# Batched x·yᵀ in fp32: two of twelve loads issued among the stores, and the first four result tiles placed after loads 6 to 9

## The chip, the core and the metric

The kernel runs on one core of a Trainium2 chip. The metric is the device time of one execution in microseconds; the time before is 301.36 us, the median of 3 runs (301.17 to 301.5). The engines of the core that matter here are PE (matmul), ACT (ScalarE), DVE (VectorE), POOL (GpSimd) and SP (SyncE, which only issues transfers here); 16 DMA engines move data between the device's memory and the core's own.

## The reference

```python
def setup_inputs():
    batch, n_heads, seq_t, seq_s, channels = 8, 12, 512, 512, 64
    return {
        "x": np.random.randn(batch, n_heads, seq_t, channels).astype(np.float32),
        "y": np.random.randn(batch, n_heads, seq_s, channels).astype(np.float32),
    }

def reference(x, y):
    return np.einsum('bhtc,bhsc->bhts', x, y).astype(np.float32)
```

For each of the 96 pairs of batch and head (called heads below) it is the product of a 512 x 64 matrix with the transpose of another, 512 x 512 out. The inputs are 12.6 MB each, the output is 100.7 MB.

## The kernel before

**Tiling.** The 96 heads are cut into six groups of 16 (`NG`, `G`). x of one group is 2 MB, and so is y of one group; each is one load of 128 partitions x 4096 fp32. There are twelve loads, numbered n = 0 to 11: even n is x of group n // 2, odd n is y of that group, so loads 10 and 11 are x and y of the sixth group. A group is worked in two halves of 8 heads (i = 0 to 11, `NH`), a half in four result tiles of 2 heads (o = 0 to 47, `V` = 4 tiles in a half). A result tile is again 128 x 4096 fp32, 2 MB, and is stored with one transfer.

**Slots.** All 60 transfers, loads and stores alike, go through five buffers of 2 MB, `slot0` to `slot4`. `slot()` (line 131) hands them out in turn, in the order in which the program asks, so whoever asks takes the buffer that was handed out five requests before, and has to wait until that one's use is over: a load waits for the conversions of the load before it or for the store before it, an eviction likewise.

**From a load to a tile.** `compress(n)` (line 144) converts a load to bf16 and frees its slot. For x it is one ACT instruction over the whole slot (line 121). For y it is four quarters in the order of `in_front` (line 116): DVE, POOL, DVE, ACT. `mix(i, name, part)` (line 168) spreads x of half i over the block layout `xbs`, four parts, and `transposes(i)` (line 183) turns `xbs` and the y copy on DVE into `xT` and `yT`, which PE multiplies. There are two of each of `xbs`, `xT` and `yT`, one for even halves and one for odd.

**Results.** `result(o, s)` (line 242) makes tile o in slot s: PE fills two PSUM buffers, `pms[0]` and `pms[1]`, with four matmuls each, and ACT evicts each of them into one half of the slot (line 249). Then the tile is stored: by SP at once, or, where `by_act(o)` (line 229) holds (every third tile and the last four), by ACT. A store by ACT is put aside in `later` and is issued between the two evictions of the next tile (lines 256 to 258), so that ACT's queue does not stand still for it.

**Order.** Every engine runs its instructions in the order in which the program emits them; `emit` (line 92) works out the semaphore waits from what is read and written. `all_products` gives PE the same order of tiles in a loop, so PE is held only by ACT's evictions and DVE's transposes. The order of the front is the loop of line 285 over n, one round per load: `compress(n)`, one part of a `mix` on POOL, a further load in the rounds 0 to 4, and so on. Loads 0 to 4 are issued ahead of it. The slots of the front come out so:

| what asks | slot | freed by |
|---|---|---|
| loads 5 to 9 | 0 to 4 | conversion of loads 0 to 4 |
| tile 0 (asks in round 5, made in round 8) | 0 | conversion of load 5 |
| load 10 (round 6) | 1 | conversion of load 6 |
| tile 1 (asks in round 7, made in round 9) | 2 | conversion of load 7 |
| load 11 (round 8) | 3 | conversion of load 8 |
| tile 2 (asks in round 9, made in round 10) | 4 | conversion of load 9 |
| tile 3 (round 11, ahead of the conversion of load 11) | 0 | store of tile 0 |

After the front comes the loop of line 303 over tiles 4 to 47, which calls `prepare(i)` (line 264) behind the last tile of each half: the transposes for the half after next, and on DVE the four parts of `mix` for the one after that.

Of the kernel before, what the change touches and what calls it, by code (L numbers as in the profile page):

```python
# [9 lines left out]
def kernel(  # L10
# [31 lines left out]
    V = G // 4  # L42
# [3 lines left out]
    SLOTS = 5  # L46
# [45 lines left out]
    def emit(name, make, reads=(), writes=(), dma=None, lane=None, known_by=None):  # L92

        points = [writer[r] for r in (*reads, *writes) if r in writer]
        points += [v for w in writes for v in readers.get(w, ())]
        if name == "pool" and name in ticks:
            points.append((name, ticks[name]))
        need(name, points, known_by)
        p, step = (lane or name, 1) if dma is None else (f"dma{dma}", 16)
        if p not in sems:  # L100
            sems[p] = tc.alloc_semaphore(p)
        if make is not None:
            make().then_inc(sems[p], step)
        at = (p, ticks.get(p, 0) + step)
        ticks[p] = at[1]
        snaps[at] = {**known[name], p: at[1]}
        if dma is None:
            for q in lanes.get(name, (name,)):
                snaps[at][q] = ticks.get(q, 0)
        for r in reads:  # L110
            readers.setdefault(r, []).append(at)
        for w in writes:
            writer[w], readers[w] = at, []
# [4 lines left out]
    def copy(name, dst, src, reads, writes):  # L118
        emit(
            name,  # L120
            lambda: nc.scalar.activation(dst, src, COPY)  # L121
            if name == "act"
            else engines[name].tensor_copy(dst, src),  # L123
            reads,
            writes,
        )

    def both(i):
        return [("slot", i, 0), ("slot", i, 1)]

    def slot():
        made_slots.append(len(made_slots) % SLOTS)
        return made_slots[-1]

    def load(n):
        i = loaded[n] = slot()
        emit(
            "sp",
            lambda: nc.sync.dma_start(slots[i], (yv if n % 2 else xv)[n // 2]),  # L139
            writes=both(i),  # L140
            dma=i,
        )

    def compress(n):

        i = loaded.pop(n)
        g = n // 2
        if n % 2 == 0:
            xk = g % (NG - 1)
            dst = xks[xk].rearrange("p r c -> p (r c)")  # L150
            copy("act", dst, slots[i], both(i), [("xk", xk)])
            return
        ys = slots[i].rearrange("p (r c) -> p r c", c=C)
        for half in range(2):
            b = g % (NG - 1 + half)
            yv2 = ybs[half][b].bitcast(bf16).rearrange("p (j c w) -> p j w c", j=R // 2, w=2)
            for ch in range(2):
                copy(
                    in_front[2 * half + ch],
                    yv2[ch * 64:(ch + 1) * 64],  # L160
                    ys[half * 64:(half + 1) * 64, :, ch * D:(ch + 1) * D].rearrange(
                        "p (j w) c -> p j w c", w=2
                    ),
                    both(i),
                    [("yb", half, b, ch)],
                )

    def mix(i, name, part):

        g, half = divmod(i, 2)  # L170
        ch, u = divmod(part, 2)
        lo = half * 64 + u * D
        xk = g % (NG - 1)
        xv2 = xbs[half].bitcast(bf16).rearrange("p (k e c u) -> p k e c u", k=K, e=E, u=2)
        copy(
            name,
            xv2[part * D:(part + 1) * D, :, :, :, u],
            xks[xk][lo:lo + D, :, ch * D:(ch + 1) * D].rearrange("p (e k) c -> p k e c", k=K),
            [("xk", xk)],
            [("xb", half, part)],  # L180
        )

    def transposes(i):
        g, half = divmod(i, 2)
        b = g % (NG - 1 + half)
        emit(
            "dve",
            lambda: nc.vector.transpose(  # L188
                xTs[half].rearrange("p (k r e) -> p k e r", k=K, e=E),
                xbs[half].rearrange("p (k e c) -> p k e c", k=K, e=E),  # L190
            ),
            [("xb", half, part) for part in range(4)],
            [("xT", half)],
        )
        emit(
            "dve",
            lambda: nc.vector.transpose(  # L197
                yTs[half].rearrange("p (r j) -> p j r", r=D),
                ybs[half][b].rearrange("p (j c) -> p j c", c=D),
            ),  # L200
            [("yb", half, b, ch) for ch in range(2)],
            [("yT", half)],
            lane="tr",
        )

    def products(o, k):
        evicted = 2 * o + k // 4 + 1
        emit("pe", None, [("xT", o // V % 2), ("yT", o // V % 2)], [("pm", k // 4)],
             known_by=[("ev", evicted), ("tr", o // V + 1)])
# [19 lines left out]
    def by_act(o):  # L229
        return o % 3 == 2 or o >= V * NH - V  # L230

    def store(o, s):
        i, h = divmod(o, V)
        name = "act" if by_act(o) else "sp"
        emit(
            name,
            lambda: engines[name].dma_start(ov[i, h], slots[s]),
            reads=both(s),
            dma=s,
        )  # L240

    def result(o, s):

        for k in range(0, K, 4):
            pm = k // 4
            products(o, k)
            emit(
                "act",
                lambda: nc.scalar.activation(  # L249
                    slots[s][:, k * S:(k + 4) * S], pms[pm].rearrange("p j s -> p (j s)"), COPY  # L250
                ),
                [("pm", pm)],
                [("slot", s, pm)],
                lane="ev",
            )
            if k == 0:
                while later:
                    store(*later.pop())
        if by_act(o):
            later.append((o, s))  # L260
        else:
            store(o, s)

    def prepare(i):

        if i < NH:
            transposes(i)
        if i + 1 < NH:
            for part in range(4):
                mix(i + 1, "dve", part)  # L270

    with tc.tile_critical():  # L272
        sems["ev"] = tc.alloc_semaphore("ev")
        ticks["ev"] = 2
        nc.scalar.sem_inc(sems["ev"], 2)
        for g in range(SLOTS):
            load(g)
        for half, name in enumerate(("dve", "pool")):
            emit(
                name,  # L280
                lambda: engines[name].memset(xbs[half], 0.0),  # L281
                writes=[("xb", half, part) for part in range(4)],
            )
        front = []
        for n in range(2 * NG):
            if n == 11:
                result(3, slot())
            compress(n)
            mix(n // 4, "pool", n % 4)
            if n == 4:  # L290
                transposes(0)
            if n < 5:
                load(n + SLOTS)
            elif n in (6, 8):
                load(n // 2 + 7)
            elif n < 10:
                front.append(slot())
            if n > 7 and n < 11:
                result(n - 8, front[n - 8])
            if n == 9:  # L300
                transposes(1)
        prepare(2)
        for o in range(V, V * NH):
            result(o, slot())
            if o % V == V - 1:
                prepare(o // V + 2)
        store(*later.pop())
        all_products()
        for i, name in enumerate(("dve", "pool", "dve", "pool", "act")):
            need(name, [(f"dma{i}", ticks[f"dma{i}"])])  # L310
# [30 lines left out]
```

## Time and profile before

| | us |
|---|---|
| median of 3 runs | 301.36 |
| the profiled execution | 301.07 |
| its span, first to last instruction | 299.2 |
| ACT busy (109 instructions) | 210.8 |
| DVE busy (73) | 151.8 |
| PE busy (384 matmuls) | 127.0 |
| POOL busy (23) | 56.1 |
| ACT, one eviction of half a tile (x96) | 1.884 |
| ACT, conversion of x (x6) | 3.617 |
| ACT, a quarter of y (x6) | 2.462 |
| DVE, a quarter of y (x12) | 3.018 |
| POOL, a quarter of y (x6) | 2.973 |

125.85 MB are moved, at 421 GB/s over the span. The transfers on SP's queue take 69.3% and those on ACT's queue 29.6% of the time of all 16 DMA engines. The median time from the issue of a transfer to its landing is 16.6 us for a store by SP, 14.7 us for a store by ACT, 17.5 us for a load of x and 20.8 us for a load of y, where one of these transfers alone is a few microseconds of the engines' time: most of it is waiting behind others. A row of a timeline gives the start, the busy time, the engine, the line, the operation with what it writes and reads, and in brackets the idle time before it and what ended that. Neighbouring instructions of one kind are merged in a row ("x2"), with their busy time added up.

### The profile page before, as it was taken

What the parts mean: (1) busy time and instruction counts of PE and PEld (TensorE: products, weight loads), DVE (VectorE), ACT (ScalarE), POOL (GpSimd) and SP (SyncE); (2) the same over time, 40 slices, a digit from 0 to 9 for tenths busy, and PEclk for the clock granted to TensorE, in tenths of its full rate; (3) what the DMA queues carried; (4) which work ended last, traced back from release to release, by engine and by line L of the source; (5) the groups of instructions that cost most, each with busy time, mean ns of one, the idle gap of its engine ahead of it and who ended that gap; (6) DMA issues with size and microseconds to landing.
All of it is one profiled execution on the core that took longest, in us unless ns stands there. A gap on an engine that the chain in (4) does not pass through costs nothing.

```text
span 299.2 us, 1282 instructions
## 1 busy us (share of the span) xinstructions
PE 127.0 (42%) x384; PEld 34.5 (12%) x384; DVE 151.8 (51%) x73; ACT 210.8 (70%) x109; POOL 56.1 (19%) x23
## 2 busy tenths in 40 slices
PE   0000040546666554565554556454646454736000
PEld 0000010111111111111111111111111111111000
DVE  2257897999839592920946729229276340000000
ACT  1665576999999886767686868585959595959400
POOL 2399999991000000000000000000000000000000
PEclk9999999958799979695979595979595979596855
DMA  7999999999999999999999999999999999999995
GB/s 274 427 431 429 434 423 429 431 429 431 429 434 429 429 431 435 425 431 436 429 431 428 434 429 429 434 425 434 434 423 427 425 434 427 425 423 429 431 429 223
DMA packets 8642, 125.85 MB, mean 421 GB/s; under 512 B 960, under 2 KB 960, under 8 KB 960
## 3 DMA queue, kind: packets, MB, share of 16 engines
q1 hardware_dynamic: 6048, 88.08, 69.3%
q10 hardware_dynamic: 2592, 37.75, 29.6%
q14 instruction: 2, 0.02, 0.0%
HBM read 25.17 MB, written 100.66 MB: 420 GB/s over the span
## 4 chain that ended last, share of the span: by engine, by line
DMA 57%; ACT 23%; PE 6%; issue 6%; DVE 2%; SPq 0%; ACTq 0%
DMA out_dram<-slot 44%; ACT slot L249 20%; DMA slot<-in_y_dram 7%; DMA slot<-in_x_dram 6%; PE pm L223 6%; DVE yb L123 2%; ACT xk L121 1%; ACT yb L121 1%; SPq L139 0%; ACTq L85 0%; SPq L336 0%; SPq L272 0%
## 5 line engine op out<-in xcount | busy, mean ns | idle before, releaser
L249 ACT ACTIVATE slot<-pm 128x2048 f32<-128x2048 f32 x96 | 173.2, 1884 | 46.9 <-DMA out_dram<-slot 43.9
L223 PE MATMUL pm<-yT,xT 128*128 128x512 bf16 x384 | 127.0, 470 | 150.5 <-ACT slot L249 113.4
L188 DVE STREAM_TRANSPOSE xT<-xb 128x2048 uint32<-128x2048 uint32 x12 | 46.7, 3890 | 71.5 <-PE pm L223 69.1
L223 PEld LDWEIGHTS pm<-yT,xT 128*128 128x128 bf16 x384 | 34.5, 111 | 242.5 <-ACT slot L249 170.9
L123 DVE COPY xb<-xk 32x2048 bf16<-32x2048 bf16 x36 | 46.9, 1303 | 1.0
L123 DVE CAST yb<-slot 64x2048 bf16<-64x2048 f32 x12 | 36.2, 3018 | 16.7 <-DMA slot<-in_y_dram 16.5
L123 POOL COPY xb<-xk 32x2048 bf16<-32x2048 bf16 x12 | 36.2, 3019 | 10.3 <-ACT xk L121 9.5
L121 ACT ACTIVATE xk<-slot 128x4096 bf16<-128x4096 f32 x6 | 21.7, 3617 | 16.1 <-DMA slot<-in_x_dram 16.1
L197 DVE STREAM_TRANSPOSE yT<-yb 128x1024 uint32<-128x1024 uint32 x12 | 23.1, 1925 | 0.0
L121 ACT ACTIVATE yb<-slot 64x2048 bf16<-64x2048 f32 x6 | 14.8, 2462 | 5.1 <-DMA slot<-in_y_dram 5.1
L123 POOL CAST yb<-slot 64x2048 bf16<-64x2048 f32 x6 | 17.8, 2973 | 1.3 <-DMA slot<-in_y_dram 0.8
L281 DVE MEMSET xb<- 128x2048 uint32 x1 | 1.8, 1765 | 1.4 <-SPq L272 1.4
L121 ACT ACT_TABLE_LOAD x1 | 1.3, 1283 | 1.0 <-SPq L272 1.0
L281 POOL MEMSET xb<- 128x2048 uint32 x1 | 1.8, 1806 | 0.5 <-SPq L272 0.5
L325 POOL MEMSET const-float32-0.0<- 128x1 f32 x1 | 0.1, 98 | 0.2 <-issue 0.2
L325 POOL MEMSET const-float32-1.0<- 128x1 f32 x1 | 0.1, 98 | 0.0
L325 POOL MEMSET const-bfloat16-1.0<- 128x1 bf16 x1 | 0.1, 98 | 0.0
L325 POOL MEMSET const-uint8-127<- 128x1 uint8 x1 | 0.1, 98 | 0.0
## 6 DMA issues: line engine op xcount, KB each, us to landing
out_dram<-slot SPq DMA_DIRECT2D x30, 2048.0 KB, 16.6
out_dram<-slot ACTq DMA_DIRECT2D x18, 2048.0 KB, 14.7
slot<-in_x_dram SPq DMA_DIRECT2D x6, 2048.0 KB, 17.5
slot<-in_y_dram SPq DMA_DIRECT2D x6, 2048.0 KB, 20.8
```

What stands on the lines that cost most here:

```text
L121: lambda: nc.scalar.activation(dst, src, COPY)
L123: else engines[name].tensor_copy(dst, src),
L188: lambda: nc.vector.transpose(xTs[half].rearrange("p (k r e) -> p k e r", k=K, e=E), xbs[half].rearrange("p (k e c) -> p k e c", k=K, e=E),),
L197: lambda: nc.vector.transpose(yTs[half].rearrange("p (r j) -> p j r", r=D), ybs[half][b].rearrange("p (j c) -> p j c", c=D),),
L223: last = nc.tensor.matmul(pms[pm][:, b, :], xT[:, 4 * pm + b, h, :], yT[:, h * S:(h + 1) * S], start=True, stop=True,)
L249: lambda: nc.scalar.activation(slots[s][:, k * S:(k + 4) * S], pms[pm].rearrange("p j s -> p (j s)"), COPY),
L281: lambda: engines[name].memset(xbs[half], 0.0),
L325: nc = _bacc.Bacc("TRN2", target_bir_lowering=False, num_devices=1)
```

## The change

Loads 10 and 11 leave the front. Rounds 6 to 9 of the front each make one of tiles 0 to 3, right behind the conversion of that round's load, in slots 0 to 3. Rounds 10 and 11 keep only their part of `mix` on POOL. In the loop over the tiles, load 10 is issued ahead of tile 16 and converted ahead of tile 20, and load 11 is issued ahead of tile 26 and converted ahead of tile 30; each takes a turn among the slots. Tile 20 is made in the slot of load 10, and tile 30 in the slot of load 11.

```diff
-        front = []
         for n in range(2 * NG):
-            if n == 11:
-                result(3, slot())
-            compress(n)
+            if n < 10:
+                compress(n)
             mix(n // 4, "pool", n % 4)
             if n == 4:
                 transposes(0)
             if n < 5:
                 load(n + SLOTS)
-            elif n in (6, 8):
-                load(n // 2 + 7)
-            elif n < 10:
-                front.append(slot())
-            if n > 7 and n < 11:
-                result(n - 8, front[n - 8])
+            if n > 5 and n < 10:
+                result(n - 6, slot())
             if n == 9:
                 transposes(1)
         prepare(2)
         for o in range(V, V * NH):
+            for n, at in ((10, 4 * V), (11, 6 * V + 2)):
+                if o == at:
+                    load(n)
+                if o == at + SLOTS - 1:
+                    compress(n)
             result(o, slot())
```

## The prediction, made before the changed kernel had run

> **What bounds the kernel now.** I read the slices first, then the engine rows at the place that the diff touches. In the slices, DMA is the busy share of the 16 transfer engines and GB/s what they moved, in 40 slices of 7.48 us.
>
> ```profile
> DMA  7999999999999999999999999999999999999995
> GB/s 274 427 431 429 434 423 429 431 429 431 429 434 429 429 431 435 425 431 436 429 431 428 434 429 429 434 425 434 434 423 427 425 434 427 425 423 429 431 429 223
> HBM read 25.17 MB, written 100.66 MB: 420 GB/s over the span
> L249 ACT ACTIVATE slot<-pm 128x2048 f32<-128x2048 f32 x96 | 173.2, 1884 | 46.9 <-DMA out_dram<-slot 43.9
> ```
>
> The reader is to see that no slice between the first and the last is below nine tenths, at about 429 GB/s, whether it holds loads (the first eight) or stores (the rest). A transfer of 2 MB (2.097 MB) at 429 GB/s is 4.89 us, and 60 of them are 293.4 us of the 299.2 us span; the remaining 5.8 us lie before the first packet and after the last. Transfers are the bound from end to end, and ACT, the busiest engine, waits 43.9 us for stores to free slots. The byte count does not change, so the question is only whether the engines ever run dry in the new order. There is nothing to gain inside the stream, as it has no hole.
>
> Next the rows of the front: ACT's, then DVE's from two windows (the two casts of load 7 together, which follow the last cast of load 5 on that engine; then the second of them alone, and the first of load 9), and SP's first two issues.
>
> ```profile
> 33.00 2.48 ACT L121 ACTIVATE yb<-slot 64x2048 bf16<-64x2048 f32 x1 [1.27 <-DMA slot<-in_y_dram]
> 37.90 3.62 ACT L121 ACTIVATE xk<-slot 128x4096 bf16<-128x4096 f32 x1 [2.41 <-DMA slot<-in_x_dram]
> 42.79 2.45 ACT L121 ACTIVATE yb<-slot 64x2048 bf16<-64x2048 f32 x1 [1.28 <-DMA slot<-in_y_dram]
> 47.69 3.62 ACT L121 ACTIVATE xk<-slot 128x4096 bf16<-128x4096 f32 x1 [2.44 <-DMA slot<-in_x_dram]
> 51.21 3.63 ACT L249 ACTIVATE slot<-pm 128x2048 f32<-128x2048 f32 x2
> 54.86 2.46 ACT L121 ACTIVATE yb<-slot 64x2048 bf16<-64x2048 f32 x1
> 57.35 3.65 ACT L249 ACTIVATE slot<-pm 128x2048 f32<-128x2048 f32 x2
> 61.02 3.62 ACT L121 ACTIVATE xk<-slot 128x4096 bf16<-128x4096 f32 x1
> 64.54 3.63 ACT L249 ACTIVATE slot<-pm 128x2048 f32<-128x2048 f32 x2
> 68.38 1.88 ACT L249 ACTIVATE slot<-pm 128x2048 f32<-128x2048 f32 x1 [0.21 <-PE pm L223]
> 68.39 0.66 ACTq L237 DMA_DIRECT2D out_dram<-slot  x1
> ```
>
> ```profile
> 43.36 6.88 DVE L123 CAST yb<-slot 64x2048 bf16<-64x2048 f32 x2
> ...
> 46.79 3.45 DVE L123 CAST yb<-slot 64x2048 bf16<-64x2048 f32 x1
> 52.59 1.33 DVE L123 CAST yb<-slot 64x2048 bf16<-64x2048 f32 x1 [2.34 <-DMA slot<-in_y_dram]
> ```
>
> ```profile
> 0.96 0.39 SPq L139 DMA_DIRECT2D slot<-in_x_dram  x1
> 1.41 0.42 SPq L139 DMA_DIRECT2D slot<-in_y_dram  x1
> ```
>
> The ACT rows that waited for a load started when it landed: load 6 at 37.90, load 7 at 42.79, load 8 at 47.69, 4.89 us apart. The store of tile 2 (by_act, line 230) goes out on ACT's queue, and line 256 puts it behind the first eviction of tile 3: it was issued at 68.39, 0.01 us after that eviction began at 68.38. This is the step on which the case turns.
>
> **The change part by part.** (1) Loads 10 and 11 leave the front. By the slices the first eight hold 3278 GB/s x 7.48 us = 24.52 MB at 59.84 us. Twelve transfers are 25.17 MB; the missing 0.65 MB take 1.5 us, so the twelfth ends at 61.35 us. Before, that twelfth transfer is load 11 and the store of tile 0 follows it without a hole. After, the first twelve are ten loads and the stores of tiles 0 and 1, and the store of tile 2 has to be in the queue by 61.35. The tenth ends 9.78 us earlier, at 51.6, the eleventh at 56.5.
>
> (2) The first tiles move ahead, each behind one conversion on ACT. I follow ACT with the durations above. Tile 0 goes into slot 0, which DVE's second cast of load 5 frees; it ends as the first cast of load 7 begins, at 43.36 (ACT is free from load 6 at 41.52). Then: tile 0 43.4 to 47.0 (3.63); ACT's quarter of load 7, 2.45, to 49.5; tile 1, 3.65, to 53.1; load 8, 3.62, to 56.75; tile 2, 3.63, to 60.4; ACT's quarter of load 9, 2.46, to 62.9; first eviction of tile 3 at 62.9. Slot 1 was freed by ACT itself, slot 2 by DVE's last cast of load 7 at 46.79 + 3.45 = 50.2, slot 3 by ACT: no wait there. PE refills a buffer in at most 1.9 us after its eviction, and between two evictions of one buffer lie 3.6 us and more: no wait there either. So tile 0's store is issued at 47.0, tile 1's at 53.1, tile 2's not at 60.4, when it is complete, but at 62.9.
>
> (3) How long an issue needs to become traffic in an empty queue is shown once, at the start. SP's first issue begins at 0.96; in quarter-microsecond windows the first packets lie in 1.75 to 2.00, so 1.05 us. The windows 2 to 4 moved 262 GB/s and not 429, which is another 0.78 us lost: 1.82 us until the effective full rate. Store 0 (47.0 against 51.6) and store 1 (53.1 against 56.5) are in time by either. Store 2 becomes traffic at 62.9 + 1.05 = 63.95 or, with the ramp, at 64.75. **The hole is 63.95 - 61.35 = 2.6 us to 64.75 - 61.35 = 3.4 us.** I take 3.0, the middle, as a store's ramp is not shown and ACT's issue instruction is longer than SP's (0.66 against 0.39).
>
> Beside the row stands a rule: the Trainium skill, DMA: Bandwidth & Descriptors, Specifications, gives about 0.6 us from issue to first byte for transfers issued by SP and ACT. By it the hole would be 62.9 + 0.6 - 61.35 = 2.15 us; the one start that this trace shows took 1.05 us, and I keep that.
>
> (4) After the hole. Tile 3's second eviction ends at 66.65 and its store (SP) is issued then, with first packets at 67.7; store 2 runs to at least 68.8. Tile 4 needs DVE's transposes of the second half, which in the trace end at 61.16 + 1.97 = 63.1 and depend on nothing that moves; PE refills after tile 3's first eviction (64.8 + 1.9), ACT evicts 66.9 to 70.5, and its store's packets can begin at 71.6, against 73.7. From there ACT makes a tile in 3.65 us and the engines take 4.89 for one, so the queue deepens by 1.2 us per tile and the wait is back on the transfers. The margin is thinnest at store 3, 1.1 us.
>
> (5) POOL loses its cast of load 11 (2.46) in the front, DVE its two casts there (6.62 us), ACT 3.62 and 2.50 us. They come back in the loop. All of it is beside the transfers, before and after, and saves nothing.
>
> (6) Load 10 in the loop, ahead of tile 16. It takes a slot as soon as that slot's store has landed, 0.33 us of SP's time, in SP's queue ahead of store 16, whose slot comes free only later; nothing on SP is held up. ACT converts it (3.62) ahead of tile 20, so what is queued behind that wait on ACT is tile 20's eviction and store, and all after. Four stores (16 to 19) stand behind the load when it lands. Count three of them to be safe: 14.7 us, less 1.5 us as a landing comes after its packets (load 0's packets end, with the ramp, near 2.8 + 4.9 = 7.7 and ACT starts on it at 8.57; 1.5 is on the safe side), 13.2 us of cover. The conversion and tile 20's two evictions take 7.3, and packets follow at 8.3 or 9.1. It costs nothing, with 4 us to spare.
>
> (7) Load 11 ahead of tile 26: DVE casts two quarters, POOL one, ACT one, ahead of tile 30. On DVE the casts stand behind the transposes and four copies for the next halves (3.9 + 1.9 + 4 x 1.3 = 11.1 us), which start when PE is through tile 27, some 10 us before the load lands: up to 2 us late. A cast is 1.33 us with POOL quiet and 3.45 beside it, so 2.7 to 6.9 us; I take 4.8, as load 9's two together were. Slot free after at most 2 + 6.9, store 30 issued 3.65 later at 12.6, against 13.2 by three stores and 18 by four. The cost is nothing at the value taken (10.5), and at the far end 12.6 + 1.8 - 13.2 = 1.2 us.
>
> (8) The tail has the same 60 uses of the five slots, the last four stores on ACT's queue, and ACT idle after 280 us: nothing moves but the whole.
>
> Sum: +3.0 us against the profiled execution's 301.07 us (span 299.2): 304.1. The median of the runs shown, 301.36, lies 0.29 above that execution, so I predict **304.3**.
>
> **The rivals.** *No hole, time as before.* This needs store 2 in the queue by 60.3, when it becomes traffic at 61.35; ACT would have to be 2.6 us earlier at tile 3. The one wait in the chain is tile 0's for slot 0, 1.84 us from 41.52 to 43.36; were that cast quicker by all of it (load 9's first took 1.33), 0.75 us of hole remain by the lower bound, 302.1. To vanish, the issue on ACT's queue would also have to pass the conversion of load 9 ahead of it, as it needs only the evictions; at 60.4 it would be traffic at 61.45 and the time 301.4. Against it: at 68.39 the issue came with the eviction that follows, not at 68.17 where tile 2's evictions ended. Chance 0.09.
>
> *A second hole in the loop* at load 10 or 11, from the point where the wait for a converted slot outlasts the stores behind it. For it: both conversions stand ahead of an eviction in ACT's order. Against: 4 us of spare in (6), 0 to 7 in (7), and ACT's 43.9 us of waiting. Price 1.2 us by (7), and 4.9 if a store more is missing: 305.5 to 309.2. Chance 0.12.
>
> *Faster, through loads that run beside stores.* Before, all loads come first; if a read and a write together moved more, two loads of some 20 us each in the queue would gain. For it: nothing. Against: the slices of loads (423 to 434) and of stores (423 to 436) are alike, and the slice where they meet, the ninth, is 429. At the best slice's 436 the gain is 40 us x 7/429 = 0.65 us, which leaves 303.6; to end below 301.36 the pair would need 8% more, 463 GB/s. Chance of ending faster 0.03.
>
> **How the numbers follow.** One hole, 2.0 to 4.0 us (the bounds 2.6 and 3.4, with the rounding of the drain and of ACT's chain, 0.6, on both sides): 303.4 to 305.4, chance 0.76. A measurement of this kernel tells 0.2%, 0.6 us, from no change. The 0.09 without a full hole split into same 0.07 and slower 0.02; so faster 0.03, same 0.07, slower 0.76 + 0.12 + 0.02 = 0.90. The range reaches down to the quick-cast case at 302.1, rounded up to 302.4, and up to 306.2, over the 1.2 us of (7): about 0.17 lie outside it.
>
> **What would show it.** In the changed profile: tile 0's eviction at 43.4; two evictions and one conversion in turn on ACT; the first issue on ACT's queue at 62.9, not 68.39; the 2 us windows between 61.4 and 64.4 nearly empty where before they move 418 to 434 GB/s; all slices after that at 429; the ACT rows after 280 us of before about 3 us later; no empty window where loads 10 and 11 are converted. I am wrong if the windows from 61 to 65 are full, or if the hole is there and the end does not move, or if a window in the loop is empty.

## The result, and the profile after

The changed kernel takes 303.80 us (median of 4 runs, 303.62 to 303.91) against 301.33 for the kernel before in the same series: a ratio of 1.0082, 95% interval 1.0069 to 1.0094. It is 2.47 us slower. The profiled execution has a span of 301.8 us against 299.2.

From the page of the changed kernel, the slices (7.545 us each now) and ACT's evictions:

```profile
DMA  7999999989999999999999999999999999999995
GB/s 278 421 441 423 426 443 413 428 341 449 419 417 436 432 416 417 447 352 415 421 441 423 436 432 422 441 423 439 426 432 434 423 439 423 434 434 421 443 423 252
HBM read 25.17 MB, written 100.66 MB: 417 GB/s over the span
L249 ACT ACTIVATE slot<-pm 128x2048 f32<-128x2048 f32 x96 | 173.0, 1892 | 46.2 <-DMA out_dram<-slot 39.5
```

The bytes are the same, and ACT still waits for stores. Two slices are low, not one: the ninth (60.4 to 67.9 us) with 341 GB/s and the eighteenth (128.3 to 135.8 us) with 352. Against 429 they lack 88/429 x 7.545 = 1.55 us and 77/429 x 7.545 = 1.35 us. The two slices differ in kind, which the DMA row hints at (8 in the ninth, 9 in the eighteenth) and narrower windows show. The columns are the window, its length, busy time and instructions of each engine, PE's granted clock, the busy share of the DMA engines, and GB/s. First the ninth slice of the changed kernel:

```profile
61.00:61.50 0.50, 0.50 (x3) 0.23 (x2) 0.50 (x2) 0.50 (x1) 0.50 (x1) 0.50 0.84 360
61.50:62.00 0.50, 0.50 (x3) 0.04 (x1) 0.50 (x1) 0.50 (x1) 0.50 (x1) 0.50 0.09 33
62.00:62.50 0.50, 0.45 (x2) 0.00 (x0) 0.50 (x1) 0.50 (x1) 0.45 (x1) 0.62 1.23 524
...
66.50:67.00 0.50, 0.24 (x1) 0.13 (x2) 0.50 (x1) 0.50 (x2) 0.00 (x0) 0.50 0.08 33
67.00:67.50 0.50, 0.50 (x2) 0.15 (x1) 0.50 (x1) 0.50 (x1) 0.00 (x0) 0.50 0.01 0
67.50:68.00 0.50, 0.50 (x2) 0.15 (x1) 0.50 (x1) 0.50 (x1) 0.00 (x0) 0.50 0.77 328
```

Here the engines run out of work twice. A window counts a packet where it starts, and a packet of 16 KB mostly takes 0.61 us, so the idle time begins about that much later than the windows look empty. By the starts and ends of the packets in the trace, the 16 engines are idle for 0.37 us on average around 62.0, between the stores of tiles 1 and 2, and for 0.96 us from 67.1 to 67.9, between those of tiles 2 and 3. That is 1.33 us in all; the kernel before has 0.01 between 58 and 75 us. Then the eighteenth slice and, 57 us later, the time at which load 11 runs:

```profile
128.00:130.00 2.00, 0.15 (x1) 0.13 (x2) 0.00 (x0) 2.00 (x2) 0.00 (x0) 0.50 1.06 451
130.00:132.00 2.00, 2.00 (x5) 0.43 (x4) 0.00 (x0) 1.79 (x2) 0.00 (x0) 0.50 1.13 344
132.00:134.00 2.00, 1.80 (x5) 0.44 (x4) 0.00 (x0) 2.00 (x2) 0.00 (x0) 0.50 0.91 336
134.00:136.00 2.00, 1.42 (x7) 0.49 (x6) 0.00 (x0) 2.00 (x2) 0.00 (x0) 0.98 0.99 311
136.00:138.00 2.00, 1.27 (x7) 0.33 (x5) 1.38 (x1) 2.00 (x2) 0.00 (x0) 1.00 0.96 385
...
190.00:192.00 2.00, 0.70 (x3) 0.21 (x3) 1.97 (x2) 2.00 (x2) 0.00 (x0) 1.00 0.99 426
192.00:194.00 2.00, 1.24 (x5) 0.41 (x5) 1.94 (x3) 1.30 (x1) 0.00 (x0) 1.00 0.97 418
```

Here the engines are busy all the time and yet move only 311 to 344 GB/s: the packets themselves take longer. Busy share over rate gives the mean time of a packet of 16 KB: 0.61 us in the row of 426, 0.83 in that of 311. ACT began to convert load 10 at 141.46, straight after a wait for it. Load 11, among stores just the same, lost nothing.

What opened the two holes of the front is in ACT's and SP's rows:

```profile
43.51 3.65 ACT L249 ACTIVATE slot<-pm 128x2048 f32<-128x2048 f32 x2 [1.86 <-DVE yb L123]
47.18 2.48 ACT L121 ACTIVATE yb<-slot 64x2048 bf16<-64x2048 f32 x1
...
56.88 3.62 ACT L249 ACTIVATE slot<-pm 128x2048 f32<-128x2048 f32 x2
60.53 2.51 ACT L121 ACTIVATE yb<-slot 64x2048 bf16<-64x2048 f32 x1
60.72 0.66 ACTq L237 DMA_DIRECT2D out_dram<-slot  x1
63.06 5.42 ACT L249 ACTIVATE slot<-pm 128x2048 f32<-128x2048 f32 x3
```

```profile
66.73 4.40 SPq L237 DMA_DIRECT2D out_dram<-slot  x2
```

ACT runs four tiles and three conversions without a pause, as predicted to within 0.2 us. The store of tile 2 is issued at 60.72, 0.2 us after tile 2's last eviction and 2.3 us before the first eviction of tile 3, behind which the program has it. Its first packet starts at 62.04; the last of tile 1's store had started at 61.54. Tile 3's store is issued at 66.73, when tile 3's second eviction is over, and its first packet starts at 67.92; tile 2's last had ended at 67.20. The rest of the front's loss is there.

### The profile page after: what moved, and what is told of

Read it like the earlier page. It is cut to its first block, busy times and chain, and to the rows that moved or that the text cites. A ratio compares the mean times of both kernels' runs of the same rounds, so it can differ in the third digit from the quotient of the medians.

```text
span 301.8 us, 1272 instructions
## 1 busy us (share of the span) xinstructions
PE 125.3 (42%) x378; PEld 34.2 (11%) x384; DVE 150.2 (50%) x73; ACT 210.7 (70%) x109; POOL 56.2 (19%) x23
## 4 chain that ended last, share of the span: by engine, by line
DMA 56%; ACT 18%; POOL 6%; PE 6%; issue 5%; DVE 2%; SPq 0%; ACTq 0%; POOLq 0%
DMA out_dram<-slot 35%; ACT slot L249 17%; DMA slot<-in_y_dram 16%; PE pm L223 6%; DMA slot<-in_x_dram 5%; POOL xb L123 4%; POOL yb L123 2%; DVE yb L123 2%; ACT xk L121 1%; SPq L139 0%; SPq L237 0%; ACTq L85 0%; POOLq L85 0%; SPq L335 0%; SPq L272 0%
## 5 line engine op out<-in xcount | busy, mean ns | idle before, releaser
L223 PE MATMUL pm<-yT,xT 128*128 128x512 bf16 x378 | 125.3, 467 | 154.8 <-ACT slot L249 116.9
L123 DVE CAST yb<-slot 64x2048 bf16<-64x2048 f32 x12 | 34.3, 2860 | 19.9 <-DMA slot<-in_y_dram 19.6
L123 POOL CAST yb<-slot 64x2048 bf16<-64x2048 f32 x6 | 18.9, 3146 | 134.0 <-DMA slot<-in_y_dram 133.5
L123 POOL COPY xb<-xk 32x2048 bf16<-32x2048 bf16 x12 | 35.3, 2940 | 10.4 <-ACT xk L121 9.6
```

Of the source, the lines that this page charges most:

```text
L223: last = nc.tensor.matmul(pms[pm][:, b, :], xT[:, 4 * pm + b, h, :], yT[:, h * S:(h + 1) * S], start=True, stop=True,)
```

## The experiments

The question is whether both slices are costs of the new order, which edit each belongs to, and what slows load 10. All times are medians beside runs of the kernel before on the same chip (301.16 to 301.22 us). A ratio is taken over the executions of both kernels and need not be that of the two medians where these scatter. The edits are against the changed kernel unless another is named.

**The changed kernel again.**

> The changed kernel once more, unaltered, for a second profile. In its first one two slices lie below the others: 341 GB/s at 60.4 to 67.9 us, worth (429 - 341)/429 x 7.545 = 1.55 us, and 352 at 128.3 to 135.8 us, worth 1.35 us. Theory A (front and load 10: both are lasting costs of the new order) expects both slices low again. Theory C (front alone: the second slice was an accident of that one execution) expects the first low and the second at 420 or more, with the time still some 2.5 us over before.

303.81 us in its one run (before: 301.22). The ninth slice has 332 GB/s and the eighteenth 339; no other slice between the first and the last is below 410. The idle time in the front is about 1.45 us (1.33 in the first profile). Both slices are lasting. Theory C fell.

**Load 10 in the front, load 11 among the stores.** The load fills the place where the engines ran dry.

```diff
             if n > 5 and n < 10:
                 result(n - 6, slot())
+            if n == 7:
+                load(10)
...
-            for n, at in ((10, 4 * V), (11, 6 * V + 2)):
+            if o == 6:
+                compress(10)
+            for n, at in ((11, 6 * V + 2),):
```

> Load 10 is issued in the front, behind tile 1's store, where the transfers ran dry; load 11 stays ahead of tile 26. A (1.5 us lost in the front, about 1.2 at load 10 among the stores, nothing at load 11): the hole is filled and no load 10 is among the stores, so 301.3 to 301.6, no slice low. B (every load among stores costs, about 1.2 us each, the front is hidden): 302.6. C (front alone, 2.5): 301.3 to 301.6.

302.05 us (301.47 to 302.51), ratio 1.0023 (1.0013 to 1.0032). The front's hole is gone, and now load 11 is slow: the slice at 180 to 188 us, where load 10 no longer runs ahead of it, falls to 359. A expected nothing at load 11 and missed that. The order of the slots shows something else here: tile 3 is now made in the slot of load 9, so its first eviction has to wait for ACT's quarter of that load, and the issue of tile 2's store comes with the eviction:

```profile
60.66 2.55 ACT L121 ACTIVATE yb<-slot 64x2048 bf16<-64x2048 f32 x1
63.32 1.88 ACT L249 ACTIVATE slot<-pm 128x2048 f32<-128x2048 f32 x1
63.34 0.66 ACTq L237 DMA_DIRECT2D out_dram<-slot  x1
```

**Load 11 in the front, load 10 among the stores.** As above, with `load(11)` in round 7, `compress(11)` in round 11, and load 10 ahead of tile 16.

> Load 11 is issued in the front, behind tile 1's store, and converted behind tile 3; load 10 stays ahead of tile 16. A: front filled, load 10 still among the stores: 302.4 to 302.7, with one low slice near 130 us. B: 302.6 as well. C: 301.3 to 301.6 and no low slice.

302.26 us, ratio 1.0032 (1.0020 to 1.0044): under A's figure, above C's. Slices of 401 and 366 at 128 to 143 us.

**The two late loads in the other order.**

```diff
-            for n, at in ((10, 4 * V), (11, 6 * V + 2)):
+            for n, at in ((11, 4 * V + 2), (10, 6 * V + 2)):
```

> Both loads among the stores, in the other order: load 11 ahead of tile 18, load 10 ahead of tile 26 (each converted four tiles later). If the slow stretch belongs to the first load after a long run of stores, it now stands where load 11 runs, near 140 us, and the time is 303.8 as the change's; if it belongs to load 10, it stands near 180 us, 303.8 too; if to its place in the sequence of stores (tile 16), it is gone, 302.6. C: 303.8 with no low slice but that of the front.

303.84 us, ratio 1.0085 (1.0068 to 1.0102). The slices of this kernel, 7.55 us each:

```profile
GB/s 276 425 436 425 425 438 419 430 336 441 428 417 425 443 416 417 447 421 382 362 434 432 423 441 426 434 428 434 428 425 441 425 434 430 434 430 425 441 425 271
```

The stretch moved with the first late load, to 136 to 151 us (382 and 362), and load 10, second now, has none. So it belongs neither to load 10 nor to tile 16: of the two loads in the loop the first is slow.

**A quarter of load 7 from ACT to POOL.** It takes 2.5 us out of ACT's chain in the front and leaves both loads where the change has them.

```diff
                 copy(
-                    in_front[2 * half + ch],
+                    "pool" if n == 7 and half and ch else in_front[2 * half + ch],
```

> The changed kernel with one quarter of load 7 moved from ACT to POOL in the front: ACT reaches tiles 1 to 3 some 2.5 us sooner, so that the store of tile 3 is issued at about 64.3 and not 66.8, ahead of the point at which the transfers run dry (66.2 us if they never stopped before). Theory A (holes of the front 1.3 to 1.5 us, slow stretch at the first load among the stores 1.0 to 1.2 us): 302.2 to 302.5, no hole at 61 to 68, the slow stretch near 130 us stays. Theory B (the holes are covered by later work and the loads alone cost): 303.8. Theory C (holes alone): 301.2 to 301.4.

302.31 us (302.21 to 303.63), ratio 1.0050 (1.0035 to 1.0066): by the medians 1.5 us less than the change, by the ratios (1.0082 against 1.0050) 1.0 us; two of the six executions took 303.04 and 303.63. Tile 2's store went out at 58.31, and in the windows of the half microseconds that stood empty the engines move on:

```profile
61.50:62.00 0.50, 0.00 (x0) 0.00 (x0) 0.50 (x1) 0.50 (x1) 0.50 (x1) 0.50 1.16 492
...
66.50:67.00 0.50, 0.48 (x2) 0.00 (x0) 0.00 (x0) 0.50 (x1) 0.50 (x1) 0.50 1.09 459
67.00:67.50 0.50, 0.26 (x1) 0.13 (x2) 0.00 (x0) 0.50 (x2) 0.48 (x1) 0.50 1.15 492
```

The idle time of the engines between 58 and 75 us is 0.01 us. So the holes come from ACT's chain, and they cost 1.0 to 1.5 us. A stands here; B and C fell.

**Loads 10 and 11 sooner, and both edits together.** `((10, 2 * V), (11, 4 * V + 2))` in the loop, alone and with the quarter on POOL.

> Load 10 ahead of tile 8 and load 11 ahead of tile 18, so that some 40 us lie between the packets of load 9 and load 10, where the change has 80, and some 53 between load 10 and load 11. Pause theory (the stretch comes where reads have paused for 75 us or more; load 11, 57 us after load 10, had none): no slow stretch anywhere, only the holes of the front: 302.6. First-load theory (the first load behind the first stores is slow whatever the pause): a slow stretch near 92 us, 303.8.

303.98 us, ratio 1.0099 (1.0082 to 1.0116).

> Both edits of the two kernels above: quarter of load 7 on POOL, loads 10 and 11 ahead of tiles 8 and 18. A with the pause theory: both costs are gone, 301.2 to 301.4, no slice between the first and the last under 415. First-load theory: 302.3.

301.96 us, ratio 1.0034 (1.0024 to 1.0044). In both, the first late load is slow, some 40 us after load 9: in the first kernel the slices at 91 to 106 us have 384 and 386, in the second those at 90 to 105 us have 400 and 383. The pause theory fell, and a shorter pause doesn't save it: in the first kernel load 10 starts 44 us after the packets of load 9 and is slow (0.70 us a packet), and load 11 starts 43 us after those of load 10 and is not (0.63). The holes of the front are worth 303.98 - 301.96 = 2.0 us in this pair, more than the 1.15 us for which the engines are idle in the first kernel.

**Load 10 in the front, load 11 ahead of tile 14.**

> Load 10 in the front behind tile 1's store, as in the kernel that ran at 302.05, but load 11 ahead of tile 14 and not 26: some 58 us between the packets of the two loads, not 115. Pause theory: no slow stretch, 301.2 to 301.4. First-load theory: slow stretch near 125 us, 302.05.

301.70 us, ratio 1.0022 (1.0013 to 1.0032), between the two figures expected. Slices of 416 and 409 at 120 to 135 us, worth (13 + 20)/429 x 7.5 = 0.6 us: the first load of the loop is slow again, but less so.

**Both loads in the front.** Load 10 behind tile 1's store and load 11 behind tile 3's; converted ahead of tiles 5 and 7.

```diff
             if n > 5 and n < 10:
                 result(n - 6, slot())
+            if n in (7, 9):
+                load(n // 2 + 7)
...
+            if o in (5, 7):
+                compress(o // 2 + 8)
```

> Tiles 0 to 3 behind loads 6 to 9 as in the change, but load 10 behind tile 1's store and load 11 behind tile 3's, so that neither runs among the stores of the loop. Two-cost theory (holes of the front; loads late among the stores, 0.5 to 1.1 us): no hole, as load 10 fills it, and no late load: 301.2 to 301.4, every slice at 415 or more. If the order of the tiles itself cost something: 301.7 or more.

301.22 us against 301.16, ratio 1.0002 (0.9992 to 1.0011). So the early place of tiles 0 to 3 costs nothing by itself. The slice at 59.9 to 67.4 us has 409, a little under the 415 expected. Both loads have stores before and behind them here, and yet the time is that of before: not every load between stores costs something. It is also no gain: of all kernels tried none beats the one before.

**A small load ahead, and all but the last four stores on SP's queue.** Both start from the kernel with the quarter on POOL (302.31). The first adds a load of 64 KB ahead of tile 12 that nobody reads; the second has `return o >= V * NH - V` in `by_act`.

> The kernel with a quarter of load 7 on POOL (302.31, no hole in the front, slow stretch of load 10 at 128 to 135 us), with one more small load: 64 KB of y of the sixth group into a tile of its own ahead of tile 12, some 20 us before load 10 runs. Over all runs the first full load among the stores was slow and a second one was not. If it is a state of the reading path that any first read clears: the stretch near 130 us is gone, 301.2 to 301.5. If it takes a full load, or has nothing to do with being first: slice near 350 as before, 302.3.

302.67 us, ratio 1.0053 (1.0037 to 1.0070); the slice at 128 to 135 us has 333. This small read clears nothing.

> The same kernel (302.31) with all stores but the last four issued by SP, so that ACT's queue holds nothing that can interleave with a load. Queue theory (the second load is quick because stores of ACT's queue alternate with its packets, and slow where SP's queue is alone): both loads are slow, near 130 and near 190 us, 303.3 or more. First-load theory: only the one near 130 us, about 302.3.

302.63 us, ratio 1.0060 (1.0037 to 1.0083), and 354 and 413 at 128 to 143 us, 419 or more in every slice after that but the last: one slow load, not two. The queue theory fell.

**Both late loads in a row.** Same base; loads 10 and 11 both ahead of tile 16.

```diff
-            for n, at in ((10, 4 * V), (11, 6 * V + 2)):
-                if o == at:
-                    load(n)
-                if o == at + SLOTS - 1:
-                    compress(n)
+            if o == 4 * V:
+                load(10)
+                load(11)
+            if o in (4 * V + 3, 5 * V):
+                compress(o - 9)
```

> The kernel with a quarter of load 7 on POOL (302.31; slow packets in two bursts, at 129 and at 133 to 135 us, about one transfer apart), with load 11 directly behind load 10, both ahead of tile 16; load 10 is converted ahead of tile 19, load 11 ahead of tile 20. Boundary theory (the bursts are the passing from stores to loads and back to stores): first burst near 129, the second one transfer later than there, near 138 to 140, and none between. First-load theory (the first load itself is slow, its end included): bursts near 129 and 133 to 135 as there, none later. About 302.3 by either.

302.21 us, ratio 1.0036 (1.0024 to 1.0049). The windows of the base (load 10 alone):

```profile
128.00:130.00 2.00, 1.72 (x4) 0.43 (x4) 0.00 (x0) 2.00 (x2) 0.00 (x0) 0.50 1.07 369
130.00:132.00 2.00, 1.94 (x5) 0.44 (x4) 0.00 (x0) 1.79 (x2) 0.00 (x0) 0.50 1.01 410
132.00:134.00 2.00, 1.42 (x5) 0.47 (x6) 0.00 (x0) 2.00 (x3) 0.00 (x0) 0.81 1.05 328
134.00:136.00 2.00, 1.27 (x6) 0.42 (x7) 0.95 (x1) 2.00 (x2) 0.00 (x0) 1.00 0.95 344
```

and of this kernel (two loads in a row):

```profile
128.00:130.00 2.00, 1.96 (x5) 0.56 (x6) 0.00 (x0) 1.79 (x2) 0.00 (x0) 0.50 0.99 303
130.00:132.00 2.00, 1.80 (x5) 0.41 (x4) 0.00 (x0) 2.00 (x2) 0.00 (x0) 0.50 0.88 360
132.00:134.00 2.00, 1.49 (x6) 0.48 (x6) 0.00 (x0) 2.00 (x2) 0.00 (x0) 0.90 1.01 434
134.00:136.00 2.00, 1.27 (x7) 0.41 (x5) 0.00 (x0) 2.00 (x2) 0.00 (x0) 1.00 1.03 385
136.00:138.00 2.00, 1.27 (x7) 0.31 (x4) 0.00 (x0) 1.15 (x1) 0.00 (x0) 1.00 0.97 279
```

There are two slow places in each. Which transfer runs in them can be counted: a transfer is 128 packets of 16 KB on one queue, taken here in the order of issue. The landings fit that: in the pair 15 of the 16 engines were through with load 10 at 136.4, the last at 139.2.

| | load 10 alone | two in a row |
|---|---|---|
| packets of load 10 | 130.1 to 138.1 | 130.1 to 136.2 |
| packets of load 11 | | 135.3 to 145.2 |
| store 17 (ACT's queue) issued, first packet | 130.21, 134.6 | 133.64, 138.1 |
| first slow place, in store 15 | 128.5 to 130.1, 0.82 us a packet | 128.0 to 130.1, 0.85 |
| second slow place | 132.0 to 134.6, in load 10, 0.84 | 135.0 to 138.1, in the end of load 10 and the start of load 11, 0.85 |

The first slow place is the end of the last store ahead of a load, the second the stretch of loads just ahead of the next store's first packet. With load 11 behind it, load 10 runs at 0.61 us a packet from 131 to 135, where alone it was slow; so the first-load theory falls. The second place has moved by 3 us, not by a whole transfer as the boundary theory expected; it goes with store 17, which was issued 3.4 us later. So what is slow here goes with the passing from one to the other, and not with load 10 as such. Why the engines slow down there is not shown.

## Why the prediction was right, and where it was not

The time, 303.80 against 304.3 forecast, and the sign were right, and so was the bound: the engines had no hole before, so a hole anywhere comes out at the end. The number is in part luck: the hole in the front was 1.3 us of idle time and not 3.0, and 1.1 us came from a place that the sum had at nothing. By the prediction's own signs, the windows from 61.4 to 64.4 were not nearly empty (62 to 64 moved 500 GB/s), and not all slices behind the front were at 429 (352).

- *Steps (1) and (2), the drain and ACT's chain:* tile 0 at 43.51 (43.4), tile 2 at 56.88 (56.75), tile 3 at 63.06 (62.9), the engines begin to fall idle at about 61.6 (61.35). Right.
- *Step (2), "tile 2's not at 60.4, when it is complete, but at 62.9":* wrong, and this is the step that failed. The issue came at 60.72, while ACT was still busy with load 9's quarter. The row it was read from, 68.39 beside an eviction that began at 68.38, could not tell the start of that eviction from the end of its wait, because there the eviction itself waited for PE (0.21 us, until 68.38), and the issue behind it with it. In the changed front PE's last matmul for the first eviction of tile 3 ended at 60.68 and its slot was free; the eviction had nothing left to wait for but ACT itself, and the issue behind it went out at 60.72. With load 10 in the front the same eviction had to wait for the quarter, and there the issue came at 63.34, as the prediction had it. So the sentence ahead of the prediction that every engine runs its instructions in the program's order needs an exception: this issue went out before the eviction ahead of it had begun. The first rival needed just this, but it too had nothing at store 3.
- *Step (3), from issue to traffic, and the hole of 3.0 us:* mis-sized by the step before. From 60.72 to the first packet at 62.04 are 1.32 us, within the bounds of 1.05 to 1.82. Counted from the end of the issuing instruction it is 0.66 us here (61.38 to 62.04), 0.65 for tile 3's store on SP (67.27 to 67.92) and 0.62 for the first load (1.35 to 1.97). The prediction was right that ACT's longer issue adds to the time. The Trainium skill, DMA: Bandwidth & Descriptors, Specifications, gives about 0.6 us for the first byte and doesn't say from when; the runs agree with it from the end of the issuing instruction, and not from its start, from which the prediction's 2.15 us counted.
- *Step (4), store 3 in time by 1.1 us:* wrong, as a consequence. Store 2 began 1.9 us sooner than thought (62.04 against 63.95) and so ended sooner; store 3 depends on ACT alone, came at 66.73 as forecast (66.65), and was late. Of the idle time 0.37 us lie ahead of store 2 and 0.96 ahead of store 3. The front lost 1.0 to 1.5 us in all (the kernel with the quarter on POOL), not 3.0.
- *Step (6), load 10 "costs nothing":* the wait was hidden as worked out, the DMA engines never ran dry in the loop. But at the first load in the loop the passing between stores and loads has a price of its own, 1.1 us by the medians in the kernel without holes (302.31 - 301.19) and 1.5 by the ratio. The prediction had put the opposite on record as a rival, loads and stores together gaining up to 0.65 us; its rows held reads and writes in separate stretches and one passing, in a slice of 429.
- *Step (7), load 11:* nothing, as taken. ACT waited 2.35 us for DVE's cast at 202.55, with the stores behind it still running. DVE's two casts took 4.71 us, as taken (4.8). The reading "1.33 us with POOL quiet" does not hold: POOL's own cast of load 9 ran from 52.70 to 56.24, over nearly all of that cast from 52.59 to 53.92.
- *Steps (5) and (8):* from 68 to 292 us no window of 2 us in the changed kernel has a busy share under 0.91, so the conversions in the loop and the tail hold nothing up, as said. With both loads in the front the early tiles give 301.22.

By the medians the two make 1.5 + 1.1 = 2.6, by the ratios 1.0 + 1.5 = 2.5, against 2.47 measured. That is no check of the two sizes, as both come from the one kernel between; the trace of the changed kernel has 1.33 us of idle time in the front and about 1.6 us that slow packets of store 15 and load 10 lost, a little more than the whole. The rival of a second hole in the loop had a size like this (1.2 us) but another cause, and its condition, engines without work, was not met.

**Open.** Why only the first load of the loop pays. The second did not in the changed kernel, nor with the loads exchanged, sooner, or with nearly all stores on one queue; and two loads between the stores of the front cost nothing. The length of the pause, a first read of 64 KB and the alternation of the two queues do not explain it. What remains is a description, not a cause.

## What to carry to other kernels

Where the transfers are the bound and never idle, reordering them has no hole to fill, and none of the orders tried here gained: look for the first moment at which the queue could run dry, and put a load there, which needs no engine to make it, not another store. Follow each engine's chain to the issue of the store after the one that looks late, since a gain at one store can turn up as a hole ahead of the next. And a load put among stores need not be free even when its wait is hidden; here the first one cost about 1 us, and two in a row what one does (302.21 against 302.31).

## What was not expected of the hardware

- An issue on ACT's queue went out when the wait of the instruction ahead of it was over, not when that instruction began: at 60.72, with the quarter of load 9 running from 60.53 to 63.04 and the eviction in between starting at 63.06. Where that eviction had to wait for the quarter, the issue came at 63.34.
- From the end of the issuing instruction to the first packet were 0.62 to 0.66 us in an empty queue, on SP and on ACT, for a load and for two stores.
- At the first load of the loop the DMA engines moved 279 to 344 GB/s in single windows of 2 us, with their busy share at 0.91 or more: a packet took 0.7 to 0.9 us in place of 0.61. A low rate at full share is not a hole, and issuing both loads sooner did not mend it (303.98).
